# The first block's recurrence outputs turned through DRAM, and a middle-block group of gates that makes its own weight sums

## The chip, the core and the metric

The kernel runs on one core of a Trainium2 chip. A core has five engines that run side by side: TensorE (PE; its weight loads are listed as PEld), VectorE (DVE), ScalarE (ACT), GpSimd (POOL) and SyncE (SP). Each works through its own list of instructions in an order that is fixed when the program is built, and waits at an instruction until the semaphores that it needs are set; what stands behind a waiting instruction waits with it. Transfers to and from DRAM are issued by SyncE and by GpSimd, each through its own queue. The metric is the device time of one execution in microseconds (us); shown are medians over several executions.

## The reference

One layer of a hybrid model works on 2048 prompt tokens and 64 tokens of one decode sequence, all in float32, with 1024 features:

```python
h = rms_norm(x, g_pre)
vA, bA, cA, zA, q, f, iv, zB, gA, gB = split_cols(einsum('btd,dn->btn', h, w_in))   # ten parts of 1024 columns
u = cA * vA
yA = (silu(zA) * bA * causal_conv3(u_ext, conv_w)) @ w_a_out
fg = lb + (1 - lb) * sigmoid(f)
S_new, o = hgrn2_scan(S0, silu(q) * QK_SCALE, 1 - fg, iv, log(fg))    # 8 heads of 128, chunks of 64 tokens
o = o * rsqrt(mean(o * o, axis=-1) + EPS)                             # 1/rms of each token and head
yB = ((o * g_onorm) * silu(zB)) @ w_b_out
merged = sigmoid(gA) * yA + sigmoid(gB) * yB
x = x + rms_norm(merged @ w_o, g_post)
x = x + (p @ w_ple_proj) * sigmoid(rms_norm(x, g_ple) @ w_ple_gate)
```

Per head and chunk the recurrence is a small attention: 64x64 scores of queries and keys under a causal mask, times the values, plus the queries times the carried 128x128 state. The change touches the step between `hgrn2_scan` and `yB`, and one of the eight groups of columns of `gA`/`gB`.

## The kernel before, in words

*Layout and blocks.* Features lie on the 128 partitions, tokens along the free axis. The 2112 tokens are worked in three blocks of 768, 704 and 640 columns; most operations take a block in two halves (384, 352 and 320). For each block the stages are: the gates (sigmoid of gA and gB, stored in DRAM until the merge), `path_b` (the recurrence, head by head), `path_a` (the convolution), the two output products with their merges, `w_o`, the norm and the final gate.

*Products and groups.* A float32 product is made of three matmuls in TensorE's fast format: the high half of the weights by the high half of the activations (L442), high by low (L443), low by high (L444). Two 128-column strips of weights are done together by `sgroup`, which needs seven products where the plain way takes eight. Their weights are, in this order, A11, S3, S1, S2, A12, A22 and S4, where the A are 512x128 pieces of the weights and the S are sums and differences of them. One product is 4 x 3 = 12 matmuls, one group 84. The products collect in PSUM banks (`pg`); ScalarE copies finished ones out (L456), VectorE adds others up.

*Where weights come from.* `combined` gives the seven operands of a group. A weight arrives by a SyncE load in a `raw` tile (A) or is added up by VectorE in an `s` tile (S); ScalarE casts it to its high half (L226, L273), and the low half is the difference that VectorE makes (L226) or that was stored in DRAM and is loaded again (`lo<-low`, `s<-low`). With `first` true, or with a group whose sums are not kept, `combined` loads the four A, makes the sums and stores each sum and its low half in DRAM. Otherwise `kept_w` loads sums and low halves that were stored before:

```python
w = combined(i1, i2, first or i1 not in sums, anew)
```

Sums are made by the groups of the first block, for the later blocks, and by `prepare_sums`, a generator that makes them ahead of their first use: GpSimd loads the four A (`r<-w_blk`, L379), VectorE makes the sums (L390 and its neighbours), GpSimd stores them. With `pieces` it does so one sum at a time, each `next` of it being a step called `piece`. From the middle block on the sums that `combined` stores go by GpSimd's queue (`stores[0] = G`; L331).

*Order.* The kernel is written with a framework that orders each engine's instructions when the program is built, by their place in the code and their priority (`tc.high_priority`, and `behind_all`, which puts an instruction behind given ones). In `path_b`, `head_prep` runs two groups for each of the eight heads (FF with IV: forget gates and values; ZB with QQ: output gate and queries). The attention of a head (`head_attn`, a generator per part of the block; the first block's six 128-token groups are in two parts) is cut into steps that are put into slots between the products of the following groups. `at(slot, step)` names the slot, and `hook()` runs the next one; a head has 14 slots, and in the first block 21, since a group of gates (`fills`) runs after each head's two groups there. In the later blocks seven of the eight gate groups run before `path_b`, and the last one, GB\*8+6, runs between two heads of `path_b`, after the sixth `head_prep`. The middle block's first head of `path_b` makes sums of its own for one pair (the first groups of that block run at 1029 to 1058 us); the group GB\*8+6 has its sums made ahead by five `piece` steps, one in each of the first five heads of the middle block.

*The recurrence's outputs.* Per 128-token group TensorE makes the outputs with tokens on the partitions (`p_o`). ScalarE squares them and sums each row, GpSimd makes 1/rms from that by a power (L689, into `ms`), VectorE scales the rows by it (L1182). Then they must be turned, features onto the partitions, and multiplied into the gate `z`. The blocks did this in two ways:
- First block: TensorE transposes each 128x128 piece into PSUM (L1187), and VectorE multiplies by the head's column of g_onorm and by `z` in one operation (L1191).
- Later blocks: the whole head's outputs stand in one tile `d["on"]`. `turn_o` (slot 11) turns 32x32 pieces on VectorE (L1053) and stores them by GpSimd in a DRAM tile `to` (L1055); `read_o` (slot 14, or in the next head's `head_prep`) reads them back in rows by GpSimd (L1060), which completes the turn; `scale_o` (slot 21) multiplies them into `z` (L1209). There g_onorm is already in `z`. (Pieces of 64 tokens, which only these blocks have, are transposed by TensorE.)

The values go the same way through a DRAM tile `tv` in all blocks, the keys through `tk` in the later ones. The keep step (`keep_z`) then stores `z` in DRAM by GpSimd.

*Other lines the prediction names.* L1016 multiplies the queries on VectorE, L1110 is the first matmul of the scores that needs them; L686 is VectorE's part of the row sums ahead of the power; L913 is a ScalarE operation on 768 columns; L964 a VectorE product of 768 columns.

Of the kernel before, what the change touches and what calls it, by code (L numbers as in the profile page):

```python
# [14 lines left out]
ALU = mybir.AluOpType  # L15
# [3 lines left out]
P = 128  # L19
D = 1024  # L20
KB = D // P
KH = KB // 2
# [9 lines left out]
VA, BA, CA, ZA, QQ, FF, IV, ZB, GA, GB = range(10)  # L32
W_A, W_B, W_O, W_G = 80, 88, 96, 104
# [60 lines left out]
def hybrid_step(  # L94
# [17 lines left out]
    V, A, G, T, SP = nc.vector, nc.scalar, nc.gpsimd, nc.tensor, nc.sync  # L112
# [69 lines left out]
    g_pre, g_on, g_post, g_ple = (vec[:, i, :] for i in range(4))  # L182
    cw = [vec[:, 4 + i, :] for i in range(3)]
    caus = [const.tile([P, P], I32, tag=f"caus{i}", name=f"caus{i}") for i in range(2)]
    keep = const.tile([P, BN], F32, tag="keep", name="keep")
# [750 lines left out]
    def head_prep(bl, hc, hd, first, hs, before):  # L936
        n, npair = bl["n"], bl["npair"]
# [29 lines left out]
        ka, kb, qe, z = hf(npair * CH), rt(), rt(), rt()  # L967
# [64 lines left out]
            queries()  # L1032
        with behind_all([*wrote, *powers]):
            by_token = [in_rows("tv", npair)]
            if before is not None and before["on"] is not None:
                before["ot"] = in_rows("to", npair, before["on"])
            if not first:
                by_token.insert(0, in_rows("tk", npair))
# [29 lines left out]
    def head_attn(ip, gs, d, hd):  # L1068
# [3 lines left out]
        nt, ln = len(gs), gs[0]["len"]  # L1072
        o0, n = gs[0]["off"], nt * ln
        qe, z, att = d["qe"], d["z"], atts[ip]
        single = ln < P
# [86 lines left out]
        with placed():  # L1162
            for i, g in enumerate(gs):
                dst = p_o[:, i * P : i * P + P]
                T.matmul(dst, att[:, i, :], v[:, i], start=True, stop=prevs[i] is None)  # L1165
                if prevs[i] is not None:
                    T.matmul(dst, cols(d["qx"], g), prevs[i], start=False, stop=True)  # L1167
        if not d["first"] and not single:
            d["on"] = rt(d["npair"] * P) if d["on"] is None else d["on"]
            on = cols3(d["on"][:, o0:], nt)  # L1170
        else:
            on = tile3(2)
# [6 lines left out]
            A.activation(on[rows], po3[rows], AF.Square)  # L1179
            V.tensor_reduce(ms[rows, :nt], on[rows], axis=mybir.AxisListType.X, op=ALU.add)  # L1180
        rstd_of(ms[rows, :nt], ms[rows, :nt], 1.0 / P, P - ln)
        V.tensor_tensor(on[rows], po3[rows], ms[rows, :nt].unsqueeze(2).to_broadcast([ln, nt, P]), ALU.mult)  # L1182
        yield
        p_t = ps_attn()
        with placed():
            for i in range(nt):
                T.transpose(p_t[:, i * P : i * P + P], on[:, i, :], ident)  # L1187
        c = slice(o0, o0 + n)
        turned_o = p_t[:, P - ln : P - ln + n]
        if d["first"]:  # L1190
            V.scalar_tensor_tensor(z[:, c], turned_o, g_on[:, hd : hd + 1], z[:, c], ALU.mult, ALU.mult)  # L1191
        else:
            V.tensor_tensor(z[:, c], turned_o, z[:, c], ALU.mult)
        yield

    def each(steps):
# [9 lines left out]

    def scale_o(d, hd):
        z = d["z"][:, : d["npair"] * P].rearrange("q (g i a) -> q g i a", i=4, a=32)
        V.tensor_tensor(z, d["ot"], z, ALU.mult)  # L1209

    def path_b(bl, hc, first, kept, fills, hs, lead_sums=None):


        def keep_z(hd, z):
            kept["o", hd] = spill("o", hd)
            G.dma_start(kept["o", hd], z)

        slots, base, d = {}, 0, None
        for hd in range(NH):
            d = head_prep(bl, hc, hd, first, hs, d)  # L1220
            if hd > 0 if first else hd == KH + 1:
                next(fills, None)
            assert not hooks
            attn = [head_attn(i, gs, d, hd) for i, gs in enumerate(bl["parts"])]
            keep = partial(keep_z, hd, d["z"])
            piece = lead_sums and partial(next, lead_sums, None)

            def at(slot, *steps):
                slots.setdefault(base + slot, []).extend(s if callable(s) else partial(next, s) for s in steps if s is not None)

            if first:
                late = 2 * (hd == 0)
                for step, slot in enumerate((1, 4, 7, 11)):
                    for g in attn:
                        at(slot + late - (late and step > 0), g)
                        slot += 1
                at(13 + late // 2, keep)
                for slot in (14, 16, 18) if hd else (16,):
                    at(slot, piece)
                if hd == NH - 1:  # L1240
                    for slot in range(22, 70, 4):
                        at(slot, piece)
            else:
                pairs, one = attn[:2], attn[2:]
                for slot, steps in enumerate((pairs[:1], pairs[1:], one, one, pairs, one, pairs, (piece,), one)):
                    at(slot + 2, *steps)
                at(11, partial(turn_o, d))
                at(14, partial(read_o, d))
                at(14 + 7, partial(scale_o, d, hd), keep)
            count = 14 + 7 * (first or hd + 1 == KH + 1) if hd + 1 < NH else 1 + max(slots) - base  # L1250
            for slot in range(base, base + count):
                steps = slots.pop(slot, None)
                hooks.append(partial(each, steps) if steps else None)
            base += count
# [378 lines left out]
    for bi, bl in enumerate(blocks):  # L1633
# [2 lines left out]
        segs = bl["segs"]  # L1636
        if bi == 1:
            stores[0] = G
        ahead_of = ((*range(W_A, W_A + KH), W_O, W_O + 1), (GB * 8 + KB - 2,), None)[bi]
        path_b(bl, hc, first, kept, fills, hs if first else None, ahead_of and prepare_sums(ahead_of, pieces=True))  # L1640
        run(fills)
        a = []
# [136 lines left out]
```

## Time and profile before

| | |
|---|---|
| median of 3 runs | 2563.61 us (2560.65 to 2564.55) |
| the profiled execution | 2562.26 us |
| its span, first to last instruction | 2560.2 us |
| granted TensorE clock, mean over the span | 0.998 |
| HBM read, written | 562.31 MB, 212.10 MB (302 GB/s over the span) |
| transfers issued by SyncE (q1) | 582.69 MB, 66.8% of 16 engines' span |
| transfers issued by GpSimd (q0) | 191.90 MB, 21.0% |

How the lines are read: the profile gives, for each engine, its busy time, the share of the span and the number of instructions. A row of groups or of the timeline names the engine, the source line (L442), the operation, then what it writes, "<-", what it reads, and shapes as partitions x elements; a timeline row begins with the start in us and the mean duration in us, `x4` counts like instructions in a row, and `[5.70 <-DVE r L1016]` says that the engine stood idle for 5.70 us before it, and that what ended this was VectorE's write of a tile `r` at L1016. In the rows of stretches, `a:b` is the stretch, followed by its length and the busy time and count of PE, PEld, DVE, ACT and POOL, then the granted TensorE clock (1.00 is full), then two figures of the transfers. "DMA to landing" is the time from a transfer's issue to its end.

### The profile page before, as it was taken

Reading aid. Unit: us, or ns where it says so; the run is one execution under the profiler, and the core shown is the slowest. Engines: PE = TensorE matmul, PEld = TensorE weight load, DVE = VectorE, ACT = ScalarE, POOL = GpSimd, SP = SyncE. Lnnn points to the kernel's source line nnn. Section 1 sums busy time; section 2 is a strip of 40 time slices with the busy share of each in tenths; the row PEclk is TensorE's granted clock in tenths of the full one; section 3 lists DMA queues with packets and bytes.
Section 4 is the critical chain, followed back from the end, with each engine's and each line's share of the span. In section 5 each row is a group of like instructions: output and inputs, shape, how many; then the busy total and the mean of one; then the engine's idle time right before and its main releaser. Section 6 shows DMA issues by size and latency. Waiting matters only on the chain.

```text
span 2560.2 us, 47051 instructions
## 1 busy us (share of the span) xinstructions
PE 2534.0 (99%) x16070; PEld 2518.5 (98%) x16070; DVE 1795.5 (70%) x3541; ACT 1484.1 (58%) x2880; POOL 471.0 (18%) x813
## 2 busy tenths in 40 slices
PE   9999999999999999999999999999999999999999
PEld 9999999999999999999999999999999999999998
DVE  7888888888768775567674556887447766336967
ACT  6666666554453664456664555566456665446675
POOL 2122122220022021122222221102112221001011
PEclk9999999999999999999999999999999999999999
DMA  8789888998797888979988998998899999999986
GB/s 329 246 279 320 276 287 289 330 363 302 259 347 248 270 313 267 306 254 312 328 285 309 339 386 312 334 311 312 304 306 318 323 338 319 298 298 323 337 272 202
DMA packets 371217, 777.60 MB, mean 304 GB/s; under 512 B 45911, under 2 KB 50705, under 8 KB 370977
## 3 DMA queue, kind: packets, MB, share of 16 engines
q1 hardware_dynamic: 321696, 582.69, 66.8%
q0 software_dynamic: 49280, 191.90, 21.0%
q8 instruction: 127, 2.08, 0.3%
q14 instruction: 114, 0.93, 0.1%
HBM read 562.31 MB, written 212.10 MB: 302 GB/s over the span
## 4 chain that ended last, share of the span: by engine, by line
PE 89%; issue 3%; DMA 3%; DVE 3%; ACT 1%; POOL 1%; SPq 0%; DVEq 0%; ACTq 0%; POOLq 0%
PE pg L442 19%; PE pg L444 19%; PE pg L443 19%; PE pg L593 5%; PE pg L594 5%; PE pg L595 5%; PE pg L632 3%; PE pg L633 3%; PE pg L631 3%; PE pa L1125 1%; PE pa L1165 1%; PE pa L1167 1%; PE pa L1111 1%; DMA lo<-low 1%; PE pa L1110 1%
## 5 line engine op out<-in xcount | busy, mean ns | idle before, releaser
L442 PE MATMUL pg<-r,hi 128*128 128x320 f32 (+2 forms) x3304 | 1081.8, 327 | 1.3 <-ACT hf L456 1.3
L443 PE MATMUL pg<-r,hi 128*128 128x320 f32 (+2 forms) x3304 | 1067.0, 323 | 0.0
L444 PE MATMUL pg<-r,lo 128*128 128x384 f32 (+2 forms) x2356 | 769.0, 326 | 5.1 <-DMA lo<-low 4.6
L273 ACT CAST hi<-raw 128x512 fp32r<-128x512 f32 x730 | 449.8, 619 | 494.9 <-PE pg L443 182.5
L442 PEld LDWEIGHTS pg<-r,hi 128*128 128x128 f32 x3304 | 622.3, 188 | 2.0 <-ACT hf L456 1.6
L443 PEld LDWEIGHTS pg<-r,hi 128*128 128x128 f32 x3304 | 623.2, 189 | 0.0
L444 PEld LDWEIGHTS pg<-r,lo 128*128 128x128 f32 x2356 | 442.5, 188 | 7.0 <-DMA lo<-low 6.0
L444 PE MATMUL pg<-r,s 128*128 128x352 f32 (+1 forms) x948 | 300.5, 317 | 0.8 <-DMA s<-low 0.7
L594 PE MATMUL pg<-r,hi 128*128 128x320 f32 (+2 forms) x864 | 277.5, 322 | 0.2 <-DVE r L226 0.2
L593 PE MATMUL pg<-r,hi 128*128 128x320 f32 (+2 forms) x864 | 274.9, 322 | 0.0
L226 ACT CAST hi<-raw 128x512 fp32r<-128x512 f32 x252 | 155.4, 620 | 165.2 <-PE pg L443 47.5
L226 DVE TENSOR_TENSOR r<-r,r 128x320 fp32r<-128x320 f32 (+7 forms) x354 | 209.0, 610 | 48.9 <-ACT r L226 47.7
L226 DVE TENSOR_TENSOR lo<-raw,hi 128x512 fp32r<-128x512 f32 x231 | 160.7, 698 | 78.2 <-ACT hi L226 67.6
L226 ACT CAST r<-r 128x320 fp32r<-128x320 f32 (+7 forms) x354 | 185.6, 557 | 48.2 <-DVE r L1330 8.2
L595 PE MATMUL pg<-r,lo 128*128 128x352 f32 (+2 forms) x564 | 180.9, 321 | 0.2 <-DMA lo<-low 0.2
L444 PEld LDWEIGHTS pg<-r,s 128*128 128x128 f32 x948 | 178.6, 188 | 1.6 <-DMA s<-low 1.6
L226 ACT CAST hi<-s 128x512 fp32r<-128x512 f32 x156 | 96.6, 619 | 132.1 <-PE pg L443 108.7
L632 PE MATMUL pg<-r,hi 128*128 128x384 f32 (+2 forms) x512 | 167.1, 327 | 0.1
L631 PE MATMUL pg<-r,hi 128*128 128x384 f32 (+2 forms) x512 | 166.0, 328 | 0.2 <-ACT hi L273 0.2
L594 PEld LDWEIGHTS pg<-r,hi 128*128 128x128 f32 x864 | 162.1, 188 | 1.8 <-DVE r L226 1.2
L593 PEld LDWEIGHTS pg<-r,hi 128*128 128x128 f32 x864 | 161.3, 188 | 1.2 <-ACT r L226 0.7
L456 ACT COPY hf<-pg 128x352 f32<-128x352 f32 (+2 forms) x354 | 157.1, 446 | 1.0 <-PE pg L444 0.6
(395 smaller groups left out, 4129.9 us busy)
## 6 DMA issues: line engine op xcount, KB each, us to landing
raw<-w_blk SPq DMA_DIRECT2D x577, 256.0 KB, 4.4
raw<-S SPq DMA_DIRECT2D x444, 256.0 KB, 4.7
lo<-low SPq DMA_DIRECT2D x422, 256.0 KB, 4.5
s<-low SPq DMA_DIRECT2D x308, 256.0 KB, 4.5
low<-lo SPq DMA_DIRECT2D x271, 256.0 KB, 4.0
S<-s SPq DMA_DIRECT2D x152, 256.0 KB, 3.8
low<-r POOLq DMA_DIRECT2D x54, 256.0 KB, 5.0
r<-w_blk POOLq DMA_DIRECT2D x52, 256.0 KB, 6.8
```

What stands on the lines that cost most here:

```text
L226: return A.copy(hi, src).ins, V.tensor_tensor(lo, src, hi.bitcast(F32), ALU.subtract).ins
L273: A.copy(hi, raw)
L442: add(hi[:, k, :], xhi, start=start and k == 0, stop=False)
L443: add(hi[:, k, :], xlo, start=False, stop=False)
L444: last[0] = add(lo[:, k, :], xhi, start=False, stop=k == KH - 1).ins
L456: copied = A.copy(got[n], ps[bank])
L593: add(hi[:, k, :], xhi, start=start and k == 0, stop=False)
L594: add(hi[:, k, :], xlo, start=False, stop=False)
L595: last[0] = add(lo[:, k, :], xhi, start=False, stop=k == KH - 1).ins
L631: T.matmul(ps, hi[:, k % 4, :], xhi[:, c], start=k == ks[0], stop=False)
L632: T.matmul(ps, hi[:, k % 4, :], xlo[:, c], start=False, stop=False)
L633: last[0] = T.matmul(ps, lo[:, k % 4, :], xhi[:, c], start=False, stop=k == ks[-1]).ins
```

## The change

There are three edits.

1. *First block's outputs.* They now also collect in a whole-head tile `d["on"]` and take `turn_o`, `read_o` and `scale_o`; the transposes on TensorE stay only for the pieces of 64 tokens that the later blocks have. Scaling by 1/rms is done in the first block by ScalarE, one 128x128 piece at a time out of PSUM; `scale_o` gets, for the first block only, one more ScalarE operation that multiplies the turned tile by the head's g_onorm column, ahead of VectorE's product with `z`.
2. *Their slots.* A head's attention has three steps instead of four, at slots 1, 4 and 7 (one later for the second part), `turn_o` at 11, `read_o` at 16, `scale_o` and the storing of `z` at 20; for the first head each is one later, its first step two. Before, `z` was stored at slot 13 there.
3. *Middle block's last gates.* `prepare_sums` runs only in the first block now. In the middle block the `piece` steps are gone, and the group GB\*8+6, with no kept sums, makes its sums in `combined`, as the groups of the first block do: four loads by SyncE, the sums and low halves on VectorE, the sums stored by GpSimd and the low halves by SyncE.

```diff
-            if before is not None and before["on"] is not None:
+            if before is not None and not first:
                 before["ot"] = in_rows("to", npair, before["on"])
...
-        if not d["first"] and not single:
+        if not single:
             d["on"] = rt(d["npair"] * P) if d["on"] is None else d["on"]
             on = cols3(d["on"][:, o0:], nt)
...
-        V.tensor_tensor(on[rows], po3[rows], ms[rows, :nt].unsqueeze(2).to_broadcast([ln, nt, P]), ALU.mult)
+        if d["first"]:
+            for i in range(nt):
+                A.mul(on[:, i, :], po3[:, i, :], ms[:, i : i + 1])
+        else:
+            V.tensor_tensor(on[rows], po3[rows], ms[rows, :nt].unsqueeze(2).to_broadcast([ln, nt, P]), ALU.mult)
...
-        turned_o = p_t[:, P - ln : P - ln + n]
-        if d["first"]:
-            V.scalar_tensor_tensor(z[:, c], turned_o, g_on[:, hd : hd + 1], z[:, c], ALU.mult, ALU.mult)
-        else:
-            V.tensor_tensor(z[:, c], turned_o, z[:, c], ALU.mult)
+        V.tensor_tensor(z[:, c], p_t[:, P - ln : P - ln + n], z[:, c], ALU.mult)
...
     def scale_o(d, hd):
         z = d["z"][:, : d["npair"] * P].rearrange("q (g i a) -> q g i a", i=4, a=32)
+        if d["first"]:
+            A.mul(d["on"], d["on"], g_on[:, hd : hd + 1])
         V.tensor_tensor(z, d["ot"], z, ALU.mult)
...
             if first:
-                late = 2 * (hd == 0)
-                for step, slot in enumerate((1, 4, 7, 11)):
-                    for g in attn:
-                        at(slot + late - (late and step > 0), g)
-                        slot += 1
-                at(13 + late // 2, keep)
+                late = int(hd == 0)
+                for g in attn:
+                    for slot in (1 + late, 4, 7):
+                        at(slot + late + (g is attn[1]), g)
+                at(11 + late, partial(turn_o, d))
+                at(16 + late, partial(read_o, d))
+                at(20 + late, partial(scale_o, d, hd), keep)
...
-                for slot, steps in enumerate((pairs[:1], pairs[1:], one, one, pairs, one, pairs, (piece,), one)):
+                for slot, steps in enumerate((pairs[:1], pairs[1:], one, one, pairs, one, pairs, (), one)):
...
-        ahead_of = ((*range(W_A, W_A + KH), W_O, W_O + 1), (GB * 8 + KB - 2,), None)[bi]
+        ahead_of = (*range(W_A, W_A + KH), W_O, W_O + 1) if first else None
```

## The prediction

> **What bounds the kernel now.** I read the page first, then the waits of TensorE, then the stretches that the change touches: one head of the first block, the second head of the middle block, and the middle block's last group of gates. Busy time, idle time and the chain come first.
>
> ```profile
> span 2560.2 us, 47051 instructions
> PE 2534.0 (99%) x16070; PEld 2518.5 (98%) x16070; DVE 1795.5 (70%) x3541; ACT 1484.1 (58%) x2880; POOL 471.0 (18%) x813
> PE 89%; issue 3%; DMA 3%; DVE 3%; ACT 1%; POOL 1%; SPq 0%; DVEq 0%; ACTq 0%; POOLq 0%
> ```
>
> TensorE is the bound: 26 us of the span are without a matmul. Any other engine's work is free as long as TensorE isn't made to wait for it; a gain must be TensorE work left out or a wait removed. A head of the first block (start, length, then busy time of PE, PEld, DVE, ACT, POOL, then the granted clock):
>
> ```profile
> 198.75:250.26 51.51, 51.51 (x320) 51.37 (x320) 44.34 (x87) 33.23 (x66) 12.18 (x17) 1.00 0.88 306
> ```
>
> There TensorE has no gap, VectorE has 7 us to spare and ScalarE 18, but both work in an order fixed when the program is built, so a wait in that order matters more than the busy time.
>
> **Term 1, the transposes that go: -4.2 us.** L1187 turns six 128x128 outputs per head in the first block.
>
> ```profile
> 225.04 0.34 PE L444 MATMUL pg<-r,lo 128*128 128x384 f32 x1
> 225.22 0.60 PE L1187 MATMUL pa<-ident,r 128*128 128x128 f32 x4
> 225.57 0.42 PE L442 MATMUL pg<-r,hi 128*128 128x384 f32 x1
> ```
>
> The duration (0.60) overlaps the next matmul; what four cost is the shift of the next start, 225.57 - 225.22 = 0.35, so six cost 0.52 and eight heads 4.2 us. VectorE comes out even per head: it loses its scalings from PSUM (L1182) and L1191, and gets a transpose and a product of 768 columns.
>
> ```profile
> 222.46 1.10 DVE L1182 TENSOR_TENSOR r<-pa,ms 128x512 f32<-128x512 f32 x2 [1.15 <-POOL ms L689]
> L1191 DVE SCALAR_TENSOR_TENSOR r<-pa,vec,r x16: 477/613/749, 127.7 to 487.2; 128x512 f32<-128x512 f32 x8, 128x256 f32<-128x256 f32 x8
> 214.44 1.58 DVE L1053 STREAM_TRANSPOSE r<-r 128x768 f32<-128x768 f32 x1
> 219.60 0.96 DVE L964 TENSOR_TENSOR r<-r 128x768 f32<-128x768 f32 x1
> ```
>
> Off: 1.10 + 0.75 + 0.48 = 2.3; on: 1.58 + 0.96 = 2.5. Covered by its 7 us.
>
> **Term 2, the removed sums ahead in the middle block: -8.8 us.** With the `piece` steps gone, the second head of the middle block loses these rows:
>
> ```profile
> 1108.53 1.60 POOL L379 DMA_DIRECT2D r<-w_blk  x3
> 1113.07 0.77 POOL L1060 DMA_DIRECT2D r<-to  x1
> 1116.66 0.69 DVE L390 TENSOR_TENSOR r<-r,r 128x512 f32<-128x512 f32 x1 [3.90 <-issue]
> 1121.58 0.82 DVE L1209 TENSOR_TENSOR r<-r,r 128x640 f32<-128x640 f32 x1 [1.41 <-DMA r<-to]
> 1122.32 0.88 DVE L1016 TENSOR_TENSOR r<-r,r 128x704 f32<-128x704 f32 x1
> 1123.36 0.76 PE L1110 MATMUL pa<-r,hf 128*128 128x128 f32 x2 [5.70 <-DVE r L1016]
> 1084.10 0.38 PE L1110 MATMUL pa<-r,hf 128*128 128x128 f32 x2
> 1193.45 0.38 PE L1110 MATMUL pa<-r,hf 128*128 128x128 f32 x2
> 1226.95 0.38 PE L1110 MATMUL pa<-r,hf 128*128 128x128 f32 x2
> 1123.40:1126.00 2.60, 2.60 (x13) 2.60 (x13) 2.25 (x4) 0.00 (x0) 0.00 (x0) 0.50 1.06 390
> ```
>
> VectorE stood 3.90 us at L390 for the four weight loads, and the queries (L1016) behind it came late: TensorE's longest wait, 5.70. Then its clock was 0.50. An undisturbed head takes 1226.95 - 1193.45 = 33.50; the three from 1084.10 to 1193.45 took 109.35, so this event cost 109.35 - 100.50 = 8.8. In the built order of the changed kernel L1016 stands ahead of the product that waits for the turned outputs, as in the other heads, so I expect the whole to go. Next late there is nothing that those heads don't show.
>
> **Term 3, the group's own sums: +8.4 us.** The last gates of the middle block run between heads 5 and 6 of it: 84 matmuls from 1254.54, seven products some 1.93 apart, the fifth (A12) from 1262.26.
>
> ```profile
> 1254.54 0.33 PE L442 MATMUL pg<-r,hi 128*128 128x352 f32 x1
> 1262.26 0.32 PE L442 MATMUL pg<-r,hi 128*128 128x352 f32 x1
> 1249.10 1.36 DVE L1053 STREAM_TRANSPOSE r<-r 128x640 f32<-128x640 f32 x1
> L331 POOL DMA_DIRECT2D S<-s x4: 539/543/544, 1029.3 to 1047.1; - x4
> DMA to landing us min/median/max: 3.3/5.2/5.5
> lo<-low SPq DMA_DIRECT2D x422, 256.0 KB, 4.5
> ```
>
> The sums and their low halves (eight VectorE operations of some 0.6) enter VectorE's packed order behind 1249.10. Counting them in at that pitch, S2 is ready at 1257.9, and the evictions they push back give the second and third product their banks some 1.4 late. GpSimd stores S2 at 1258.0; the store lands at 1263.2 (5.2). In SyncE's order the load of the next group's low half, which takes over that buffer, waits for this landing, and the low half of A12 stands behind it: issued near 1264.2, landed 4.5 later at 1268.7, while TensorE, 1.4 late, wants it at 1264.1. That is 4.6 + 1.4 = 6.0. The bounds: with 3.3 for the store and the sums in time 0, at 5.5 and later loads 7. The four loads, four S loads and four low loads that fall away are off the path.
>
> What a wait does to the clock is shown twice more, at 2.54 and at 1.27:
>
> ```profile
> 931.34 0.56 PE L444 MATMUL pg<-r,lo 128*128 128x352 f32 x1 [2.54 <-DMA lo<-low]
> 931.30:934.00 2.70, 2.66 (x9) 2.66 (x10) 1.27 (x2) 0.97 (x2) 0.00 (x0) 0.53 1.06 410
> 1377.34 0.43 PE L442 MATMUL pg<-r,hi 128*128 128x352 f32 x1 [1.27 <-ACT hf L456]
> 1377.30:1379.30 2.00, 1.96 (x12) 1.96 (x13) 0.29 (x2) 2.00 (x5) 0.00 (x0) 1.00 0.82 281
> ```
>
> After 2.54 the clock was 0.53 (some 1.6 lost), after 5.70 it cost 3.1, after 1.27 it stayed 1.00. For 4.6 I take 2.4, between them: 6.0 + 2.4 = 8.4. The Trainium skill, "TensorE: Matmul & The Clock Gate" (What's actually happening), has the clock halved only after an idle window of about 3.4 us; the trace differs, since 2.54 sufficed here. By that rule too the 4.6 would slow the clock, and waits of 2 to 3 us would not.
>
> **Term 4, the new wait on ScalarE: +12 us.** Per head ScalarE gets six scalings from PSUM and one of 768 columns by g_onorm (L913 is such a one); it has the time. But the last one works on what comes back from DRAM, and in the built order of heads 1 to 6 it stands right ahead of the eviction L456 and the cast of A12 for the gates group.
>
> ```profile
> 221.39 1.71 POOL L689 TENSOR_TENSOR ms<-ms,mhalf 128x4 f32<-128x4 f32 x2 [4.53 <-DVE ms L686]
> L1055 POOL DMA_DIRECT2D tv<-r x7: 540/540/588, 112.7 to 423.0; - x7
> DMA to landing us min/median/max: 3.7/4.3/4.4
> L1060 POOL DMA_DIRECT2D r<-tv x7: 771/799/809, 126.2 to 429.7; - x7
> DMA to landing us min/median/max: 4.1/4.9/6.9
> 232.20 0.62 ACT L226 CAST hi<-raw 128x512 fp32r<-128x512 f32 x1 [1.49 <-PE pg L443]
> 238.49 0.34 PE L442 MATMUL pg<-r,hi 128*128 128x384 f32 x1
> L913 ACT ACTIVATE r<-r,vec 128x768 f32<-128x768 f32 x8 | 7.5, 937 | 16.4 <-DVE r L896 16.4
> DVE r L1209 <- DMA r<-to: 46.2, 16, 6.7
> ```
>
> In the third head: the powers end by 222.4; three scalings of some 0.3 (a guess between nothing and half of L1182), an eviction and a cast bring VectorE's next low half to 225.0, a sum and an addition follow, the transpose runs 226.1 to 227.7. Store issued 228.0, landed 232.1 to 232.3, read landed 4.9 later: 237.2. ScalarE would be there near 233.7 and stands 3.5 us. Scaling 0.94, eviction 0.4, cast 0.6: the weights are ready at 239.1, the low half 0.7 after. TensorE, 0.52 ahead of the old 238.49, wants them at 238.0, and the low half at 238.3: 1.5 us late. At 4.1 for the read it is 0.7, with the store at its least too about 0; at 6.9 it is 3.5. I take 1.5 in each of the eight heads. That VectorE waited 46.2 us over 16 heads for just such reads in the other blocks shows that the built order trusts them too early; there it cost TensorE nothing but in the one head of term 2.
>
> **Sum.** -4.2 - 8.8 + 8.4 + 12.0 = +7.4. The profiled execution took 2562.26 (span 2560.2 and 2.1 around it), so 2569.7; it lies 1.35 below the median of 2563.61. On the median: 2571.
>
> **Rivals.**
> - *The reads return in time (faster side).* Each head's round trip is 1.5 us shorter, by the 4.1 row and a quicker store, and ScalarE's wait stays under the lead of its casts. Then -4.2 - 8.8 + 8.4 = -4.6: 2559. It turns faster below 0.9 us late per head. For it: of the 16 heads of the later blocks whose VectorE waited for such a read, only term 2's shows a TensorE wait for it. Against: the lead there was VectorE's, here the casts follow it at once. Chance 0.20.
> - *The reads in time and the own sums free*, as the first group of the middle block makes its own sums without a wait at 1029 to 1058: -4.2 - 8.8 + 1 = -12: 2552. Against: there the sums were done 15 us ahead. Chance 0.10.
> - *ScalarE late but the own sums free:* -4.2 - 8.8 + 1 + 12 = 0: 2564. Chance 0.18.
> - *Reads at the 6.9 end:* 3.5 late a head, and past 2.5 the clock row adds 1.6: 8 x 5.1 = 41, so +36: 2600. Against: the median is 4.9. Chance 0.08.
>
> **How the numbers follow.** Forecast 0.44, by itself 2565 to 2578. A difference under 0.2% (5.1 us) can't be told from no change. Faster: all of the second rival, half of the first, a little of the third, 0.25; same: the rest of the first, most of the third and the forecast's low edge, 0.25; slower 0.50. The range 2553 to 2588 leaves out the last rival and the tail of the second.
>
> **What would show it.** L1187 on `r` gone from TensorE's groups. In the middle block the 5.70 wait gone and its heads 33.5 apart. ScalarE idle some 3.5 us per head of the first block until a read of `to`, and TensorE waiting there for a cast or low half 0 to 3 us, eight times. One TensorE wait of 3 to 6 us near 1260 for `lo<-low`, with a clock near 0.5 behind it. It is wrong if ScalarE's wait is there and TensorE's is not, or if A12's low half is issued before 1260.

## The result and the profile after

The changed kernel takes 2602.35 us (median of 4, 2600.09 to 2608.27) against 2564.08 before: a ratio of 1.0157, 95% interval 1.0143 to 1.0171. It is 38 us slower, where 7 slower were forecast. The page of the changed kernel, lines as before: span and busy times.

```profile
span 2600.7 us, 46997 instructions
PE 2544.2 (98%) x16022; PEld 2520.8 (97%) x16022; DVE 1799.8 (69%) x3525; ACT 1496.2 (58%) x2932; POOL 482.6 (19%) x825
```

TensorE has 48 matmuls fewer, the transposes, and is yet busy for 10 us more: some of its matmuls ran longer. Its time without a matmul rose from 26.2 us (2560.2 - 2534.0) to 56.5. The waits of TensorE (line and what it waited for: sum, times, longest), then two of ScalarE:

```profile
PE pg L442 <- ACT hi L226: 13.2, 8, 4.3
PE pg L444 <- DMA lo<-low: 11.6, 4, 7.2
PE pa L1110 <- DVE att L1119: 9.1, 4, 2.8
...
ACT r L1210 <- DMA r<-to: 34.9, 7, 7.9
ACT r L1184 <- POOL ms L689: 18.1, 10, 2.2
```

L1210 is the new scaling by g_onorm, L1184 the new scaling by 1/rms. ScalarE stands at both: 34.9 us for the turned outputs to come back, 18.1 us for GpSimd's power. TensorE pays in two places, for casts that come late (13.2) and for the causal mask, VectorE's L1119 (9.1).

Where the time went is read from the first L1110 of each head, which stands at the same place in every head's work. The stretch from the first block's first head to the middle block's first one, before and after (stretch, length, then busy times of PE, PEld, DVE, ACT, POOL):

```profile
98.73:1084.10 985.37, 980.05 (x5843) 975.97 (x5842) 771.95 (x1384) 555.73 (x1070) 189.17 (x309) 1.00 0.86 294
```

```profile
98.37:1117.58 1019.21, 988.59 (x5796) 977.58 (x5795) 776.22 (x1368) 568.96 (x1126) 203.17 (x326) 0.99 0.84 291
```

It is 33.8 longer: TensorE's idle time grows from 5.3 to 30.6, and its busy time by 8.5 although the transposes are gone. The middle block from there to its last head grows from 256.5 to 258.0; what follows takes 1225.1 against 1219.6. This last 5.5 lies in many places of under 3 us, with no line that the change touches, and in the runs below the same stretch takes from 1216.3 to 1227.6. I don't assign it.

In the middle block, TensorE's one large wait (timeline: start, duration, operation, idle time before and its end):

```profile
1295.74 0.66 PE L444 MATMUL pg<-r,lo 128*128 128x352 f32 x1 [7.25 <-DMA lo<-low]
```

### The profile page after: what moved, and what is told of

The parts are those of the page before. It is cut to its first block, busy times and chain, and to the rows that moved or that the text cites. A ratio compares the mean times of both kernels' runs of the same rounds, so it can differ in the third digit from the quotient of the medians.

```text
span 2600.7 us, 46997 instructions
## 1 busy us (share of the span) xinstructions
PE 2544.2 (98%) x16022; PEld 2520.8 (97%) x16022; DVE 1799.8 (69%) x3525; ACT 1496.2 (58%) x2932; POOL 482.6 (19%) x825
## 5 line engine op out<-in xcount | busy, mean ns | idle before, releaser
L442 PE MATMUL pg<-r,hi 128*128 128x320 f32 (+2 forms) x3304 | 1084.1, 328 | 17.2 <-ACT hi L226 13.2
L444 PE MATMUL pg<-r,lo 128*128 128x384 f32 (+2 forms) x2368 | 777.6, 328 | 14.2 <-DMA lo<-low 11.6
L444 PEld LDWEIGHTS pg<-r,lo 128*128 128x128 f32 x2368 | 448.1, 189 | 19.8 <-DMA lo<-low 13.3
L444 PE MATMUL pg<-r,s 128*128 128x320 f32 (+1 forms) x936 | 296.1, 316 | 3.0 <-DMA s<-low 3.0
L444 PEld LDWEIGHTS pg<-r,s 128*128 128x128 f32 x936 | 175.7, 188 | 4.4 <-DMA s<-low 4.4
L226 DVE TENSOR_TENSOR lo<-s,hi 128x512 fp32r<-128x512 f32 x160 | 113.4, 709 | 67.8 <-ACT hi L226 58.3
```

The costliest lines, as they stand in the source:

```text
L226: return A.copy(hi, src).ins, V.tensor_tensor(lo, src, hi.bitcast(F32), ALU.subtract).ins
L442: add(hi[:, k, :], xhi, start=start and k == 0, stop=False)
L444: last[0] = add(lo[:, k, :], xhi, start=False, stop=k == KH - 1).ins
```

## The experiments

In the diffs, "-" and "+" are against the kernel that the paragraph names. Each was timed beside the kernel before on the same chip (2561.89 to 2562.96 there). An edit higher up in a file moves the line numbers: L448 of such a kernel is L444, L1111 is L1110, L1120 is L1119.

### The two parts alone

First block's outputs alone, against the changed kernel:

```diff
-                for slot, steps in enumerate((pairs[:1], pairs[1:], one, one, pairs, one, pairs, (), one)):
+                for slot, steps in enumerate((pairs[:1], pairs[1:], one, one, pairs, one, pairs, (piece,), one)):
...
-        ahead_of = (*range(W_A, W_A + KH), W_O, W_O + 1) if first else None
+        ahead_of = ((*range(W_A, W_A + KH), W_O, W_O + 1), (GB * 8 + KB - 2,), None)[bi]
```

> The first block's edits alone; the middle block keeps its sums made ahead. In the changed kernel the distance from the first L1110 (98 us) to the middle block's first one (1117.58) grew by 33.8 us. Theory A, the loss is the first block's own: 33.8 slower than before, 2594 to 2602 us, with the middle block's heads at 39.3, 36.3 and 33.8 as before. Rival B, the two parts disturb each other (a backlog carried from block to block): the first block alone loses under 25, below 2590.

Own sums alone are the same two lines the other way round, against the kernel before.

> The middle block's last gates make their own sums; the first block's outputs stay as before. Theory A: the second head loses its 5.70 wait (-9.0), the gates group gains a wait of 6 to 8 for a low half with a slow clock (+10.5), sum +1.5: 2563 to 2568 us. What the changed kernel lost behind 1376 us (+5.5) is then either the middle block's (2568 to 2572 here) or the first block's or chance (2563 to 2567). Rival B, the own sums free without the first block's disturbance: -8, 2556.

Measured: 2596.87 (ratio 1.0137, 1.0123 to 1.0151) and 2566.03 (1.0016, 1.0008 to 1.0025), that is +35.0 and +4.1. They add up to 39.1, and the whole change has 38.3: theory A in both runs, and the parts don't disturb each other. In the run with own sums alone the middle block's heads are 33.4 apart and the gates group takes 58.24 instead of 46.89 with its head.

### Who stands for the turned outputs

Against the changed kernel, g_onorm goes into `z` early, so nothing on ScalarE waits for the read:

```diff
                 A.activation(half(z, h), whole(x, y), AF.Silu)
+                A.mul(half(z, h), half(z, h), g_on[:, hd : hd + 1])
...
-        if d["first"]:
-            A.mul(d["on"], d["on"], g_on[:, hd : hd + 1])
```

> The changed kernel, but ScalarE multiplies g_onorm into the gate z right after its Silu (two operations of 384 columns a head) and nothing on ScalarE waits for the turned outputs any more. Theory A, ScalarE's wait in its fixed order is the cause: TensorE's waits for a cast ahead of A12 and for the causal mask go, with VectorE waiting at most 2 us a head in its product: 2560 to 2573 us. Rival B, the round trip through DRAM is the cause whichever engine stands for it: VectorE waits 3 to 5 us a head and the time stays above 2588.

Or the scaling and the product come some 20 us later:

```diff
-            A.mul(d["on"], d["on"], g_on[:, hd : hd + 1])
+            with behind_all(copies):
+                A.mul(d["on"], d["on"], g_on[:, hd : hd + 1])
...
-                at(20 + late, partial(scale_o, d, hd), keep)
+                at(24 + late, partial(scale_o, d, hd), keep)
```

> The changed kernel, with the scaling by g_onorm and the product behind it placed some 20 us later in ScalarE's and VectorE's orders, when the read has long landed; the same operations and transfers otherwise. Theory A (the wait): no wait at the scaling, the first block's loss of 38 goes and the 4.2 of the transposes show: 2560 to 2568 us. Rival B (VectorE and ScalarE are too full with the added work: turn 1.58, product 0.95, scalings): TensorE's waits for the causal mask (9 us in all) and the slow clock behind them stay, above 2575.

Measured: 2586.00 (1.0089, 1.0075 to 1.0104) and 2578.19 (1.0070, 1.0053 to 1.0086). The first lies between its theories. The second has the time of its rival B and that rival's sign: ScalarE's wait at the scaling is gone, but TensorE's waits for the mask stay. Whether the added work is the reason, as that rival has it, the next section tests. The first run's product (its L1210) on VectorE, by line with its idle time, then TensorE's waits in the second run:

```profile
L1210 DVE TENSOR_TENSOR r<-r,r x8: 944/945/959, 145.4 to 515.2; 128x768 f32<-128x768 f32 x8
its engine sat idle before it (us, times) until:
  DMA r<-to: 3.8, 2
```

```profile
PE pa L1110 <- DVE att L1119: 6.9, 4, 1.9
PE pg L442 <- ACT hi L226: 4.1, 2, 2.9
```

VectorE stood for the read in two of the eight heads only, 3.8 us in all, so the round trip is not lost on whichever engine stands for it; rival B of the first run falls on that. Yet with the later scaling VectorE is late for the mask. Rows around the start of the third head (start, duration), before and with the later scaling:

```profile
197.91 0.39 PE L1110 MATMUL pa<-r,hf 128*128 128x128 f32 x2
...
200.09 0.77 DVE L1119 COPY_PREDICATED att<-caus,pa 128x256 f32<-128x256 int32 x2
...
201.59 0.33 PE L1110 MATMUL pa<-r,hf 128*128 128x64 f32 x2
```

```profile
170.64 0.89 ACT L1184 ACTIVATE r<-pa,ms 128x128 f32<-128x128 f32 x3 [2.19 <-POOL ms L689]
...
171.76 0.65 ACT L226 CAST hi<-s 128x512 fp32r<-128x512 f32 x1
...
172.44 0.69 DVE L226 TENSOR_TENSOR lo<-s,hi 128x512 fp32r<-128x512 f32 x1 [2.89 <-ACT hi L226]
...
196.95 0.39 PE L1110 MATMUL pa<-r,hf 128*128 128x128 f32 x2
...
201.53 0.76 DVE L1119 COPY_PREDICATED att<-caus,pa 128x256 f32<-128x256 int32 x2
...
202.44 0.41 PE L1110 MATMUL pa<-r,hf 128*128 128x64 f32 x2 [1.66 <-DVE att L1119]
```

The first L1119 comes 2.2 us after the head's first L1110 before, and 4.6 after it here, where the second part's L1110 waits for it. In this kernel VectorE shows no gap over 0.15 from 177.4 to 202.3, and what it lost ahead of that it does not make up: it had stood 2.89 for a cast of ScalarE, which itself had stood 2.19 for the power at its 1/rms scaling. That this is the cause is tested next.

### The 1/rms back on VectorE

Against the kernel with the later scaling, and against the changed kernel:

```diff
-        if d["first"]:
-            for i in range(nt):
-                A.mul(on[:, i, :], po3[:, i, :], ms[:, i : i + 1])
-        else:
-            V.tensor_tensor(on[rows], po3[rows], ms[rows, :nt].unsqueeze(2).to_broadcast([ln, nt, P]), ALU.mult)
+        V.tensor_tensor(on[rows], po3[rows], ms[rows, :nt].unsqueeze(2).to_broadcast([ln, nt, P]), ALU.mult)
```

> The kernel with the g_onorm scaling placed later (2578.2), with the 1/rms scaling given back to VectorE, as one operation per part. Theory A: ScalarE's second in-order wait, 2.2 us a head at its first 1/rms scaling for GpSimd's power, holds back the casts for VectorE (which idles 2.9 there) and so the causal mask and TensorE behind it; with it gone the first block gains the transposes' 4.2 over the kernel with own sums only (2566.0): 2560 to 2567. Rival B, VectorE is full: 1.1 us more work a head makes the waits for the causal mask longer, above 2578.

> The changed kernel with the 1/rms scaling given back to VectorE; the g_onorm scaling stays where it waits for the read. Theory A, two waits that add up: the one at the 1/rms is worth what the run with the later scaling keeps above its floor, some 12 to 14, so 2586 to 2593 here. Rival B, the wait for the read hides the other one: within 4 of the changed kernel, 2598 to 2606.

Measured: 2567.05 (1.0018, 1.0009 to 1.0027) and 2585.95 (1.0096, 1.0079 to 1.0113). So there is a table of two by two, in us:

| | 1/rms on ScalarE | 1/rms on VectorE |
|---|---|---|
| g_onorm scaling early (waits for the read) | 2602.35 | 2585.95 |
| g_onorm scaling late | 2578.19 | 2567.05 |

Moving the 1/rms to ScalarE costs 11 to 16, the early scaling 19 to 24. (The cells weren't all timed on one chip; taken against the kernel before on the same chip, 2564.08 for the first cell and 2561.89 and 2562.20 for the others, it is 11 to 15 and 19 to 22.) Giving VectorE 1.1 us more work a head made the kernel faster, so a full VectorE is not the reason: that is theory A's cause in both runs, with both times 0.05 us outside its ranges. What didn't come is the 4.2 of the transposes over the kernel with own sums alone (2566.03). TensorE's waits in the second run, in the stretch up to the middle block:

```profile
PE pa L1110 <- ACT r L1099: 7.1, 3, 2.8
PE pg L442 <- ACT hi L226: 6.0, 6, 2.6
...
PE pa L1110 <- DVE att L1119: 1.3, 1, 1.3
```

The waits for the mask go with the 1/rms: 9.1 in the changed kernel, 6.9 with the later scaling, 1.3 here and none with both mended. What is left in this run are waits for ScalarE, its casts and its L1099. The heads of the first block with both mended:

```profile
145.99:196.79 50.80, 50.80 (x315) 50.74 (x313) 44.40 (x85) 32.50 (x64) 12.90 (x15) 1.00 0.84 292
...
299.11:353.60 54.49, 52.88 (x314) 52.17 (x313) 44.74 (x86) 32.95 (x65) 12.14 (x19) 0.97 0.84 295
```

Four of the six whole heads from 145.99 on take 50.8 where they took 51.5: the transposes were worth 0.65 a head. The kernel's fifth head (from 299.11) is 3.65 longer than its neighbours, more than five heads win, and the stretch behind the eighth start, 632.8 against 630.7 with own sums alone, does the rest. In the fifth (GpSimd, then ScalarE):

```profile
330.41 0.77 POOL L1060 DMA_DIRECT2D r<-to  x1 [3.19 <-DMA to<-r]
...
331.91 1.62 POOL L379 DMA_DIRECT2D r<-w_blk  x3
...
340.72 0.62 ACT L226 CAST r<-r 128x512 fp32r<-128x512 f32 x1 [3.64 <-DMA r<-w_blk]
```

GpSimd stood 3.19 for the landing of the turned outputs before it could issue the read, with the weight loads of the sums ahead queued behind; ScalarE stood 3.64 for these.

### GpSimd's queue in the first block

Against the kernel with both mended, the read of the turned outputs goes behind the read of the values, and so behind those loads:

```diff
+        if kind == "tv":
+            reads[:] = [read.ins]
...
         if "ot" not in d:
-            d["ot"] = in_rows("to", d["npair"], d["on"])
+            with behind_all(reads if d["first"] else ()):
+                d["ot"] = in_rows("to", d["npair"], d["on"])
```

(`read` is the DMA that `in_rows` issues; the step itself is at slot 18.)

> The kernel with the later g_onorm scaling and VectorE's 1/rms (2567.0), with GpSimd's read of the turned outputs behind its read of the values, and so behind the weight loads of the sums ahead where there are any. Theory A: GpSimd's 3.2 us stand for the store's landing held back those loads in the fifth head (54.49 against 50.82 of its neighbours) and behind the eighth; now all heads are 50.8 apart: 2559 to 2564. Rival B, the fifth head is late for its own sums' work, as before in part (52.21): within 1.5 of 2567.

Measured: 2567.44 (1.0019, 1.0011 to 1.0028), no different, which is rival B's time. (The 52.21 that the expectation names is the sixth head of the kernel before, not the fifth, which took 51.52 there.) The fifth head goes from 54.49 to 52.83, and VectorE stands in it for another transfer, a weight load of SyncE's own queue:

```profile
336.47 0.69 DVE L352 TENSOR_TENSOR s<-raw,raw 128x512 f32<-128x512 f32 x1 [2.03 <-DMA raw<-w_blk]
```

The stand for the landing was real, and taking it away moved the lateness to another load. That the two kinds of loads now compete for the transfer engines would explain it and is not shown.

### The middle block's own sums

Against the kernel with own sums alone: a fourth tile for sums, paid for with one tile of the ring (the pool of the `r` tiles),

```diff
-RING = 48
+RING = 47
...
-        return wp.tile([P, 4, P], dt, tag="s", name=nm("s"), bufs=3)
+        return wp.tile([P, 4, P], dt, tag="s", name=nm("s"), bufs=4)
```

> The kernel with own sums only (2566.0), with four tiles for sums instead of three (and one ring tile less). Theory A: TensorE's 7.5 wait in the middle block's last gates comes from SyncE standing for the landing of a sum's store, since the next low half takes over the tile; with a fourth tile SyncE issues the low half of A12 some 5 us sooner and the wait falls below 2.5: 2555 to 2560. Rival B, the load's own 7 us under full DMA sets it: the wait stays above 5 and the time at 2563 or more.

and A12 split ahead of the third sum in this group (`sooner` is true where the stores go by GpSimd):

```diff
+            sooner = stores[0] is G
+            if sooner:
+                out["A12"] = split_w(a12, (i1, 1), among_sums=True)
             s2 = total("S2", s1, a11, ALU.subtract)
-            out["A12"] = split_w(a12, (i1, 1), among_sums=True)
+            if not sooner:
+                out["A12"] = split_w(a12, (i1, 1), among_sums=True)
```

> The kernel with own sums only (2566.0), with the middle block's A12 split ahead of the third sum, so that in SyncE's order its low half stands ahead of the load that waits for the landing of a sum's store. Theory A, the place behind that load makes TensorE's 7.5 wait: the low half is issued some 5 us sooner, the wait falls to 0 to 2.5 and most of 10.5 us comes back: 2556 to 2560. Rival B, the low half takes the place of another that is then late: wait above 5, 2563 or more.

Measured: 2581.08 (1.0067, 1.0050 to 1.0085) and 2562.15 (1.0003, 0.9995 to 1.0012). The fourth tile was no test: a third low half of a sum took it, the wait fell to 5.62 only, and the kernel lost 15 us, by the fourth tile or the missing ring tile; which was not looked into. The second run's waits, in place of one of 7.5:

```profile
1259.85 0.43 PE L448 MATMUL pg<-r,lo 128*128 128x352 f32 x1 [1.70 <-DMA lo<-low]
1265.80 0.65 PE L448 MATMUL pg<-r,lo 128*128 128x352 f32 x1 [3.75 <-DMA lo<-low]
```

A12's low half now comes 1.70 late, as theory A had it, and that of A22 3.75 late, as rival B had it: the time lies between the two, and part of the loss goes back to where the queue is now longest. Both of these edits together, on the first block with the later read:

> Both of these together. If the parts add up, 2566.0 less 5 for the transposes and less 7 to 10 for the low half: 2550 to 2555, faster than both kernels. If they disturb each other: 2558 or more.

Measured: 2566.61 (1.0017, 1.0007 to 1.0028). The parts don't add up here; why is not shown.

### What made the wait that the change removed

The prediction put the middle block's 5.70 wait on the sums made ahead. Three edits against the kernel before: the loads a head earlier; the sums behind the queries; and the product of the turned outputs behind the queries.

```diff
+        lead = ahead_of and prepare_sums(ahead_of, pieces=True)
+        if bi == 1:
+            next(lead)
```

> The kernel before, with the four weight loads of the sums made ahead in the middle block issued ahead of its first head, so that the sums too come a head earlier. Theory A, VectorE's 5.70 late queries came from standing for those loads: the wait goes and the heads are 33.5 apart, 9 less: 2551 to 2555. Rival B, another wait takes its place (the sums in the first head, loads in the norm's traffic): 2559 or more.

```diff
-            piece = lead_sums and partial(next, lead_sums, None)
+            def piece():
+                with behind_all(() if first else adds):
+                    next(lead_sums, None)
+
+            piece = lead_sums and piece
```

> The kernel before, with each sum made ahead in the middle block put behind VectorE's latest addition of its head, so behind the queries (L1016), one a head; loads, stores and all operations are kept. Theory A: the 5.70 wait of the second head came only from the sums' place ahead of the queries; the heads are 33.4 apart, the gates group stays at 46.9: 9 less, 2551 to 2555. Rival B, a wait of the same size moves elsewhere, as it did with the loads issued earlier (2561): 2559 or more.

The first gave 2561.15 (0.9991, 0.9981 to 1.0001): the 5.70 is gone, and TensorE waits 3.91 at 1064.68 for a low half and 1.52 for a mask instead. The second gave 2564.17 (1.0008, 0.9999 to 1.0017), with the wait still there. Both times are their rivals'. VectorE and TensorE in the second:

```profile
1114.38 0.89 DVE L1015 SCALAR_TENSOR_TENSOR r<-r,r 128x704 f32<-128x704 f32 x1
1121.15 0.83 DVE L1209 TENSOR_TENSOR r<-r,r 128x640 f32<-128x640 f32 x1 [5.88 <-DMA r<-to]
1121.89 0.89 DVE L1016 TENSOR_TENSOR r<-r,r 128x704 f32<-128x704 f32 x1
1122.92 0.77 PE L1110 MATMUL pa<-r,hf 128*128 128x128 f32 x2 [5.34 <-DVE r L1016]
```

No sum stands there, and VectorE stands in the product for the read of the turned outputs, with the queries behind it. In the kernel before, the 3.90 at the sums (1112.76 to 1116.66) began ahead of that stand, and the product then stood for 1.41 only. The product behind the queries, on this kernel and on the one before:

```diff
-                V.tensor_tensor(qe, qe, eq, ALU.mult)
+                made = V.tensor_tensor(qe, qe, eq, ALU.mult)
+            asked[:] = [] if first else [made.ins]
...
-        V.tensor_tensor(z, d["ot"], z, ALU.mult)
+        with behind_all(asked):
+            V.tensor_tensor(z, d["ot"], z, ALU.mult)
```

> The kernel with the sums put behind (2564.2), with the product of the turned outputs and the gate put behind the queries (L1016) in VectorE's order in every head of the later blocks, as it stood in all heads but the middle block's second. Theory A: the 5.3 wait of that head is VectorE's stand for the read of the turned outputs, with the queries behind it; with both orders mended the heads are 33.4 to 34 apart and the time 9 less than before: 2553 to 2557. Rival B, the queries are late for something else again, wait above 4: 2561 or more.

> The kernel before with that product put behind the queries and the sums ahead where they were, ahead of the queries. If the stand at the sums for the four weight loads (3.90 us) has a share of its own, the wait falls from 5.7 to 2 to 4 and the time to 2556 to 2560; if the product's stand was all, the wait goes and the time is that of the run beside this.

Measured: 2558.30 (0.9979, 0.9970 to 0.9988) and 2558.66 (0.9989, 0.9979 to 0.9998). With both orders mended the wait is gone; with the product alone it is 3.13, the part of the sums:

```profile
1118.44 0.76 PE L1111 MATMUL pa<-r,hf 128*128 128x128 f32 x2 [3.13 <-DVE r L1016]
```

So either stand alone holds the queries back, the product's for 5.3, the sums' for 3.1, and they overlapped. These two kernels are some 4.5 us faster than the kernel before. Of the 9 us that were expected of the first, half came: there TensorE waits for the mask four more times, 0.6 once behind the product and 0.8 three times behind a sum, and the middle block from its first head to its last is 252.2 long, 4.3 less than before.

Last, the first block with the later read, joined to the middle block with the sums put behind:

> The same middle block, and the first block with the outputs turned through DRAM, VectorE's 1/rms, the later g_onorm scaling and the later read. Theory A, the first block's spacing (50.8 in most heads) survives and the parts add: 2551 to 2558. Rival B, what the first block saves on TensorE it loses in its fifth and eighth heads to transfers and VectorE, as the runs so far had it: the same as or slower than the kernel with the sums put behind alone, by 0 to 5.

Measured: 2566.21 (1.0018, 1.0009 to 1.0027) against 2564.17 without the first block's edits: rival B. Even with its three waits taken away, the first block's change isn't worth anything here.

## Why the prediction was wrong

The sign was right and the size was not: +7.4 forecast, +38.3 measured, outside the range. The step that failed is the first block's part of the sum, -4.2 + 12 = +7.8, where the stretch of the first block grew by 33.8: of the two waits that the change gives ScalarE, term 4 priced one, by its direct successor alone, and put the other, at the 1/rms, at nothing.

**Term 1, the transposes, -4.2.** Right, a little small. With the waits mended the undisturbed heads are 0.65 shorter, 5.2 for eight. In the changed kernel none of it shows. The rest stands one row behind the prediction's three, in the kernel before: the prediction counted the shift of the next start (225.57 - 225.22 = 0.35 for four transposes), but the matmul from 225.57 is slowed too, with 0.26 to the start behind it where 0.17 is usual.

```profile
225.83 0.34 PE L443 MATMUL pg<-r,hi 128*128 128x384 f32 x1
```

That makes 0.44 for four and, at the same rate, 0.66 for six.

**VectorE even per head, "covered by its 7 us".** Right for the work: with 1.1 more a head, in the kernel with both mended, the undisturbed heads are 50.8 apart. Wrong as a cushion for a VectorE that is late. Most of the 7 us (5.6, in gaps over 0.15) lie ahead of 222.5 in the head from 198.75 on; between the 1/rms and the next head's mask VectorE stands only twice, 0.29 and 0.89, and the mask's lead over TensorE is small (before, it ended at 200.86, and L1110 that needs its bank began at 201.59: 0.7). What is late at the 1/rms arrives at the mask.

**Term 2, -8.8.** Right in size: the heads are 33.4 apart in the changed kernel, 9.0 less over three. The cause was wrong in part: the queries were held by the product's stand for the turned outputs as much as by the sums' for their loads (5.34 remains without the sums, 3.13 without the product). The forecast came out because the removal of the `piece` steps also put the queries ahead of the product in the built order, as the prediction had read there.

**Term 3, +8.4.** Measured +10.5: the gates group and its head take 57.41 against 46.89. The place is as forecast, the queue too. SyncE in the changed kernel (the low halves of the next group, then A12's, the first of the two behind), and what SyncE waited for from 1282.5 to 1289.5:

```profile
1282.85 4.09 SPq L274 DMA_DIRECT2D s<-low  x2
...
1287.51 1.67 SPq L274 DMA_DIRECT2D lo<-low  x2
...
SPq L274 <- DMA S<-s: 3.4, 1, 3.4
SPq L274 <- PE pg L444: 0.7, 1, 0.7
```

The landing of a sum's store held the queue for 3.4, as written. A12's low half then took 8.2 from its row's start to its landing instead of 4.5, with the transfer engines busy throughout (a share of 1.00 from 1287.5 to 1295.7), and 0.7 of that was a wait for TensorE's last read of a low half. So TensorE waited 7.25 where 4.6 was forecast; the excess is in this load.

**Term 4, +12 for ScalarE's wait.** This is the term that was mis-sized. Its own mechanism came as written: ScalarE stood 34.9 in seven heads (5.0 each, forecast 3.5), and TensorE waited 13.2 in the first block for the casts behind it, against 12. But by the table, taking this wait away is worth 19 to 24. The third head's rows (ScalarE, then TensorE):

```profile
250.69 0.93 ACT L1210 ACTIVATE r<-r,vec 128x768 f32<-128x768 f32 x1 [4.95 <-DMA r<-to]
...
251.89 0.62 ACT L226 CAST hi<-raw 128x512 fp32r<-128x512 f32 x1
252.56 0.44 PE L442 MATMUL pg<-r,hi 128*128 128x384 f32 x1 [2.13 <-ACT hi L226]
```

The 33.8 of the stretch add up as -5.2 for the transposes, 13.2 for the casts, 9.1 at the mask, 3.0 in other waits, and 13.7 by which TensorE's other matmuls ran longer (its busy time is 8.5 up with 5.2 of transposes gone). The last three, 26 us, were put at nothing. The first cause behind them is ScalarE's other stand, at the 1/rms: the chain counted the three scalings as work in front of VectorE's turn, and didn't count that ScalarE waits for the power with casts behind it. By the table this is worth 11 to 16, and nearly all of the 9.1 at the mask goes with it. The second is the clock, taken as full behind waits of 1.5. From the first block's first head to 560 us it was 0.98 (1.00 in the kernel before), which by an estimate from this row is 461.63 x 0.02 = 9 of the 13.7:

```profile
98.37:560.00 461.63, 436.63 (x2580) 428.61 (x2579) 366.98 (x683) 281.67 (x588) 107.80 (x151) 0.98 0.81 283
```

The prediction itself had said that a wait in the fixed order matters more than busy time.

**The rivals.** The measured total is nearest to the rival with reads at the 6.9 end (2600, chance 0.08), by luck and not for its reason: the reads of outputs and values took 5.4 at the median and 6.4 at most.

```profile
L1060 POOL DMA_DIRECT2D r<-to x8: 756/771/773, 136.9 to 518.8; - x8
L1060 POOL DMA_DIRECT2D r<-tv x7: 758/761/799, 128.4 to 464.8; - x7
...
DMA to landing us min/median/max: 4.2/5.4/6.4
```

The rivals on the faster side fell: in seven of eight heads ScalarE stood for the read, and the own sums weren't free.

**What would show it.** Of the signs named, those for terms 1 and 2 are there. That for term 3 is, but at 7.25 the wait is longer than the 3 to 6 named. Of the eight TensorE waits for ScalarE's late cast in the first block, seven are over 1 us, one of them, 4.3, longer than the 0 to 3 named. Missing from the list is TensorE waiting for the mask.

## What to carry to other kernels

Work that moves from one in-order engine to another takes its wait with it: ask of each moved instruction what it waits for and which casts or evictions stand behind it on the new engine. Here VectorE could stand for 1/rms at 1.1 us, and ScalarE's 2.2 for the same power delayed every cast behind it; giving VectorE the work back saved 11 to 16 us. Idle time summed over a stage is no reserve for an engine that is packed just ahead of the next engine's need: measure the lead at that point, as 0.7 us here, and charge every delay beyond it.

A wait in a trace that names one releaser can have a second one hidden behind it. Take each away alone, and both together, before a gain is booked to one of them.

## What was not expected of the hardware

The clock behind a wait doesn't follow the length of the wait alone. Three waits of TensorE in the first block of the changed kernel: 2.81 ahead of 211.07, 2.13 ahead of 252.56 and 1.72 ahead of 526.18. The trace is cut here at 210.48, where a slow stretch begins, and at whole multiples of 3.413 us from there (length, then PE's busy time; the granted clock is the first figure after POOL's):

```profile
207.06:210.48 3.42, 1.21 (x8) 0.93 (x6) 3.42 (x7) 1.87 (x4) 0.73 (x2) 1.00 0.97 303
210.48:213.89 3.41, 2.82 (x12) 2.85 (x13) 1.94 (x5) 1.03 (x3) 0.34 (x1) 0.50 1.04 378
...
248.03:251.44 3.41, 2.40 (x14) 2.08 (x12) 1.31 (x3) 0.75 (x1) 2.15 (x5) 1.00 0.93 323
251.44:254.85 3.41, 2.17 (x11) 1.86 (x12) 2.31 (x4) 3.41 (x8) 0.00 (x0) 1.00 1.02 312
254.85:258.27 3.42, 3.42 (x21) 3.42 (x20) 3.42 (x7) 3.39 (x7) 2.68 (x2) 1.00 1.06 421
...
524.51:527.92 3.41, 1.63 (x8) 1.31 (x9) 1.76 (x3) 3.24 (x6) 0.54 (x1) 1.00 1.03 410
527.92:531.34 3.42, 3.42 (x12) 3.42 (x11) 3.42 (x6) 2.22 (x6) 1.14 (x3) 0.50 0.99 381
```

The slow stretches of this kernel begin on this grid and last 3.41 us or twice that. Where TensorE was without a matmul for 2.2 or 1.8 us of one such stretch, the next ran at half clock. The wait of 2.13 is split by the edge at 251.44 into 1.0 and 1.2, and the clock stays full behind it. So what counted is how much of a wait fell into one stretch of the grid. Cut in this way, the profiles of all the runs agree: all 53 changes from full to half clock, the kernels' first and last 20 us left out, lie on their run's grid. Of the stretches at full clock every one with 1.9 us or more without a matmul was followed by such a change, none with under 1.6 was, and between these figures both occur. The Trainium skill, "TensorE: Matmul & The Clock Gate" (What's actually happening), speaks of an idle window of some 3.4 us; here about half of such a length was enough.
